# A gated DeltaNet and Conformer block on one core: the long convolution's accumulator moves into PSUM, the recurrence's products share a bank, and GpSimd's queue gets an order between heads

## The chip, the core and the metric

The kernel runs on one core of a Trainium2 chip. Five engines of that core matter here: TensorE (PE, with PEld for its weight loads), VectorE (DVE), ScalarE (ACT), GpSimd (POOL) and SyncE (SP), whose queue issues most of the DMAs. Each engine works through its own instruction queue in order and waits where an instruction needs a result that isn't there yet. PE's products land in PSUM, which the kernel uses as 8 banks of 128 x 512 fp32. The metric is device microseconds (us) of one execution; the profile shows one execution, and its granted clock is the share of TensorE's full clock that the chip gave.

## What is computed

One residual block on x of 512 frames by 1024 channels, in float32: an RMSNorm, one wide input projection, two token mixers in parallel (a gated delta rule with 8 heads of 128, and a Conformer convolution), gates that merge them, an output projection, then a SwiGLU channel mixer and a last RMSNorm. Cut to the parts that the change touches:

```python
h = rmsnorm(x, norm1_w); proj = h @ w_in              # q, k, v, z, beta, decay, glu, gates
qkv = silu(causal_depthwise_conv(q|k|v, dn_conv_w))   # 4 taps
# gated delta rule, per head, in chunks: with T = I + strict lower part of beta*k k^T*decay
#   solve T [u | w] = [v*beta | k*beta*exp(gc)], then chunk by chunk
v_new = u_c - w_c @ S
o_c   = q_dec_c @ S + attn_c @ v_new
S     = S * exp(g_last) + k_dec_c^T @ v_new
out_a = (rmsnorm(o) * silu(z)) @ dn_w_o
c     = ga * sigmoid(gb)
c     = causal_depthwise_conv(c, cm_dw_w) + cm_dw_b   # 31 taps, per channel
c     = silu(layernorm(c))                            # over the 1024 channels
out_b = c @ cm_w_pw2 + cm_b_pw2
x     = x + (gate_a * out_a + gate_b * out_b) @ w_out
x     = x + (silu(h2 @ w_gate) * (h2 @ w_up)) @ w_down
```

## The kernel before

Channels lie on the 128 partitions and the 512 frames along the free axis, so one column tile of a projection is a 128 x 512 result in one PSUM bank, summed over 8 blocks of 128 input channels (a k step). Every product of the big projections is split into a high and a low part of both factors and done as three matmuls (`split3`, line 113), so a column tile is 24 matmuls. `unit` (lines 92 to 105) loads the weights of a tile by an SP DMA, makes the high part on ACT (line 102) and the low part on DVE (line 104).

The first phase runs 60 column tiles of the input projection, as generators that yield after each k step: for each of the 8 heads k, q, v and z (`head`, lines 643 to 670), with 8 k steps of other tiles (`others`: GLU tiles, then gate tiles) after each head. The driver (lines 683 to 702) takes one k step at a time and counts them; between k steps it advances the running chains of small work. A framework then turns the program into one queue per engine by priority and by its own estimates of when things are ready; `behind` (lines 85 to 90) and `tc.issue_after` put instructions of a block behind a given earlier one on that one's engine. The queues are fixed before the kernel runs.

Each head's small work has three stages.

- `front` (lines 326 to 378), once k is there. On POOL: a power (line 339), the masked products `Un` (349) and `Ud` (366), and then a forward substitution in 16 x 16 blocks, 15 pairs of a multiply (`ytm`, line 375) and an add (`y`, line 377). Between them ACT copies blocks of `Un` out (354), DVE makes `cc` (357), and SP stores `cc` to DRAM and loads it back, spread over the partitions, as `U`, in 8 DMAs (359, 362); the substitution reads `U`. `decay` (315 to 324) has one POOL instruction more per head (320).
- `front2` (380 to 397), after v: `Vp`, the masked q k products `at` (DVE, line 390) and the norms of q (PE, line 395).
- `chain` (399 to 510), from k step 84 + 40 h on: the blocks' inverse is built up to 128 x 128 (lines 405 to 464; line 405 on ACT is the first reader of the substitution's `y`, line 407 on DVE reads that, line 414 on PE reads 407's result, line 426 on DVE makes `Xd` for line 438 on PE), then the recurrence over 4 chunks of 128 frames (470 to 504). A chunk has five products: k S (476), q S (480), the inverse times R (482), the state's update (487), and `at` times w (494). Products 476 and 487 go into tile `sp`, which has a bank of its own; the other three go into slices of tile `st`, another bank. DVE makes R (478) and the new state (492), ACT makes w (484) and the scaled q S, `Ae` (499), and DVE adds the output `o` (500). In chunk 0 the state and o are ACT copies (490, 496). Both tiles have a single buffer.

The long convolution, `conv31` (lines 539 to 548), runs 8 times, once per 128 channels: ACT writes the first tap into an SBUF tile `cv[i]` (541), and 30 DVE instructions (543) each add one tap to it; each reads `c` and the accumulator and writes the accumulator, all in SBUF. `background` (615 to 621) hands them to the framework at the lowest priority, every 40 k steps, so that they fill DVE's gaps; several convolutions can be under way at once, each in its own `cv` tile. Their sum over the channels is `sacc` (545 to 548).

`ln_mean` (559 to 573) takes that sum with a matmul (561), subtracts the mean from all 8 tiles and sums the squares; it is called at the end of the first phase (708). `ln_norm` (575 to 583) needs one more matmul (577), scales, and applies SiLU on ACT (583); it is called before tile 3 of the 8 column tiles of the attention output projection (732). After those the tiles are split (725, 726) and go through the convolution branch's output projection.

Banks of PSUM in the first phase: 3 for projections (`mm`), 2 for `front` (`g`), 1 for `chain` (`b`), 1 each for `sp` and `st`.

Of the kernel before, what the change touches and what calls it, by code (L numbers as in the profile page):

```python
# [1 line left out]

# [28 lines left out]
def block_kernel(ctx, tc, a):  # L31
    nc = tc.nc
    V, S, G, PE = nc.vector, nc.scalar, nc.gpsimd, nc.tensor
# [91 lines left out]
    cv = [kp.tile([P, T], F32, name="cv", bufs=KD) for _ in range(KD)]  # L125
    tp = keep.enter_context(tc.tile_pool(name="tp", bufs=2))

    ph1 = ctx.enter_context(ExitStack())
    psg = ph1.enter_context(tc.tile_pool(name="psg", bufs=2, space=PSUM))
    psb = ph1.enter_context(tc.tile_pool(name="psb", bufs=1, space=PSUM))  # L130
    pst = ph1.enter_context(tc.tile_pool(name="pst", bufs=2, space=PSUM))

    cs = []

# [191 lines left out]
    def front(h, kT, DT):  # L326
        sq = junk[:, 0:P]

        ss = gp.tile([P, 8, NT], F32, name="ss", bufs=5)
        ps = tok(kT, psg, "g")  # L330
        for n in range(NT):
            S.activation(sq, ps[:, n, :], AF.Square, accum_out=ss[:, 0, n:n + 1])
        kd = gp.tile([P, 3, P], F32, name="kd", bufs=3)
        for n in range(3):
            S.activation(kd[:, n, :], ps[:, n, :], AF.Copy, scale=kdf[:, n, h:h + 1])
        kk, rk, nk, nb2, b2 = ss[:, 3], ss[:, 4], ss[:, 5], ss[:, 6], ss[:, 7]
        V.tensor_scalar(out=kk, in0=ss[:, 0], scalar1=EPS, scalar2=None, op0=ALU.add)
        V.reciprocal(out=rk, in_=kk)
        G.tensor_tensor(out=nk, in0=kk, in1=root4, op=ALU.pow)
        V.tensor_tensor(out=nb2, in0=rk, in1=nbeta[:, :, h], op=ALU.mult)  # L340
        V.tensor_tensor(out=b2, in0=rk, in1=beta[:, :, h], op=ALU.mult)

        ps = psg.tile([P, 4, P], F32, name="g")
        for n in range(NT):
            PE.matmul(ps[:, n, :], kT[:, n, :], kT[:, n, :], start=True, stop=True)  # L345
        Un = gp.tile([P, NT, P], F32, name="Un", bufs=3)
        for n in range(NT):
            S.activation(Un[:, n, :], ps[:, n, :], AF.Copy, scale=nb2[:, n:n + 1])  # L348
        G.tensor_tensor(out=Un, in0=Un, in1=DT, op=ALU.mult)  # L349

        cp = gp.tile([P, NT, 32], F32, name="cp")
        for b in range(4):
            b32 = slice(32 * b, 32 * b + 32)
            S.copy(out=cp[b32], in_=Un[b32, :, b32])
        cc = gp.tile([P, NT, 16], F32, name="cc")
        S.activation(cc, cp[:, :, 0:16], AF.Copy, scale=mh1)
        V.scalar_tensor_tensor(out=cc, in0=cp[:, :, 16:32], scalar=mh2, in1=cc, op0=ALU.mult, op1=ALU.add)
        sc = dram.tile([8, 16, NT, 16], F32, name="sc")
        nc.sync.dma_start(sc.rearrange("b k n c -> (b k) n c"), cc)
        U = gp.tile([P, 16, NT, 16], F32, name="U", bufs=2)  # L360
        for b in range(8):
            nc.sync.dma_start(U[16 * b:16 * b + 16].rearrange("p k n c -> p (k n c)"),
                              sc[b].rearrange("k n c -> (k n c)").partition_broadcast(16))

        Ud = gp.tile([P, NT, P], F32, name="Ud", bufs=3)
        G.tensor_tensor(out=Ud, in0=Un, in1=mc.rearrange("p (a t) -> p a t", a=1).broadcast_to([P, NT, P]),
                        op=ALU.mult)


        y = gp.tile([P, NT, 16], F32, name="y", bufs=3)  # L370
        S.copy(out=y, in_=idc.rearrange("p (a c) -> p a c", a=1).broadcast_to([P, NT, 16]))
        for k in range(15):
            w = 15 - k
            tm = gp.tile([P, NT, 16], F32, name="ytm")
            G.tensor_tensor(out=tm[:, :, 0:w], in0=U[:, k, :, k + 1:],  # L375
                            in1=y[:, :, k:k + 1].broadcast_to([P, NT, w]), op=ALU.mult)
            G.tensor_tensor(out=y[:, :, k + 1:], in0=y[:, :, k + 1:], in1=tm[:, :, 0:w], op=ALU.add)  # L377
        return ss, kd, b2, Un, Ud, y

    def front2(kT, qT, vT, DT, ss):  # L380
# [18 lines left out]
    def chain(h, kT, qT, ss, kd, b2, Un, Ud, Vp, at, yq, zs):  # L399
# [68 lines left out]
        o = gp.tile([P, NT, P], F32, name="o", bufs=3)  # L468
        Sp = None
        for n in range(NT):  # L470
            pp = pst.tile([P, P], F32, name="sp", bufs=1)
            ps = pst.tile([P, 4, P], F32, name="st", bufs=1)
            if n == 0:
                R = Vp[:, 0, :]
            else:
                PE.matmul(pp, kT[:, n, :], Sp, start=True, stop=True)
                R = gp.tile([P, P], F32, name="R", bufs=3)
                V.scalar_tensor_tensor(out=R, in0=pp, scalar=negc[:, n, h:h + 1], in1=Vp[:, n, :],
                                       op0=ALU.mult, op1=ALU.add)
                PE.matmul(ps[:, 2, :], qT[:, n, :], Sp, start=True, stop=True)  # L480
                yield 3
            PE.matmul(ps[:, 1, :], Y[:, n, :], R, start=True, stop=True)  # L482
            w = gp.tile([P, P], F32, name="w", bufs=2)
            S.activation(w, ps[:, 1, :], AF.Copy, scale=b2[:, n:n + 1])
            yield 3
            if n < NT - 1:
                PE.matmul(pp, kd[:, n, :], w, start=True, stop=True)  # L487
                Sn = gp.tile([P, P], F32, name="S", bufs=2)
                if n == 0:
                    S.activation(Sn, pp, AF.Copy)  # L490
                else:
                    V.scalar_tensor_tensor(out=Sn, in0=Sp, scalar=egl[:, n, h:h + 1], in1=pp,
                                           op0=ALU.mult, op1=ALU.add)
            PE.matmul(ps[:, 3, :], at[:, n, :], w, start=True, stop=True)  # L494
            if n == 0:
                S.activation(o[:, 0, :], ps[:, 3, :], AF.Copy)
            else:
                Ae = gp.tile([P, P], F32, name="R", bufs=3)
                S.activation(Ae, ps[:, 2, :], AF.Copy, scale=egc[:, n, h:h + 1])
# [37 lines left out]
    sacc = tp.tile([P, T], F32, name="sacc", bufs=1)  # L537

    def conv31(i, c):
        acc = cv[i]  # L540
        S.activation(acc, c[:, 0:T], AF.Identity, scale=c31w[:, i, 0:1], bias=dw_b[:, i:i + 1])
        for k in range(1, 31):
            V.scalar_tensor_tensor(out=acc, in0=c[:, k:k + T], scalar=c31w[:, i, k:k + 1], in1=acc,  # L543
                                   op0=ALU.mult, op1=ALU.add)
        if i == 1:
            V.tensor_tensor(out=sacc, in0=cv[0], in1=cv[1], op=ALU.add)
        elif i > 1:
            V.tensor_tensor(out=sacc, in0=sacc, in1=cv[i], op=ALU.add)
# [94 lines left out]
    def head(h, done):  # L643

        k_ = yield from conv4(8 + h, "kT")
        close()
        q_ = yield from conv4(h, "qT")
        close()
        v = conv4(16 + h, "vT")
        for _ in range(2):  # L650
            next(v)
            yield
        DT = dts.pop(0)
        if h + 1 < H:
            dts.append(decay(h + 1))
        with behind():
            ss, kd, b2, Un, Ud, y = front(h, k_, DT)
        v_ = yield from v
        pz = yield from proj(24 + h)
        z_ = zall[:, h, :]  # L660
        S.activation(z_, pz, AF.Silu)


        def last():
# [4 lines left out]
        chains.append([count[0] + 5, last()])  # L669
        yield  # L670

    def others():
# [8 lines left out]
            yield  # L681


    done, ended, dts, convs, count, chains = [], [], [], [], [0], [[0, decays()]]
    rest = others()
    for h in range(H):
# [17 lines left out]
    for _, sc, e in ended:  # L704
        if not sc:
            scaled(*e)
        finish(*e)
    vacc = ln_mean()
    ph1.close()


# [17 lines left out]
    mas = []  # L729
    oh, ol = zip(*[split(zall[:, k, :]) for k in range(KD)])  # L730
    for j in range(KD):
        if j == 3:
            ln_norm(vacc)
        ps = psm.tile([P, T], F32, name="mm")
        col_tile(ps, a["wo"][j], oh, ol)
        ma = mp.tile([P, T], F32, name="ma", bufs=KD + 1)
        V.tensor_tensor(out=ma, in0=ps, in1=gate_of(j), op=ALU.mult)
        mas.append(ma)
# [331 lines left out]
```

## Time and profile before

| | |
|---|---|
| median of 3 runs | 1000.03 us (997.23 to 1003.04) |
| the profiled execution | 1000.16 us |
| its span, first to last instruction | 998.4 us |
| granted clock over the span | 0.987 |
| busy: PE, DVE, ACT, POOL | 963.2, 680.7, 508.4, 302.1 us |
| long convolution on DVE (line 543) | 240 instructions, 186.5 us, mean 803 ns |
| substitution on POOL (lines 375, 377) | 240 instructions, 57.3 + 53.1 us |
| DMA over the span | 138.49 MB, mean 139 GB/s |

Rows of a time line give start and duration in us, the engine, the line of the kernel, the operation, what it writes and reads (`out<-in`), the shape and, after x, how many of them are merged in the row; in square brackets stands the idle time of the engine before it and whom it waited for. A row of waits reads "who <- for whom: total us, times, longest". Busy times of PE overlap from one matmul to the next, so a matmul's duration is longer than the step from one to the next. PE counts an fp32 product as two matmuls, so the four products of a head's small step show as x8.

### The profile page before, as it was taken

What the parts mean: (1) busy time and instruction counts of PE and PEld (TensorE: products, weight loads), DVE (VectorE), ACT (ScalarE), POOL (GpSimd) and SP (SyncE); (2) the same over time, 40 slices, a digit from 0 to 9 for tenths busy, and PEclk for the clock granted to TensorE, in tenths of its full rate; (3) what the DMA queues carried; (4) which work ended last, traced back from release to release, by engine and by line L of the source; (5) the groups of instructions that cost most, each with busy time, mean ns of one, the idle gap of its engine ahead of it and who ended that gap; (6) DMA issues with size and microseconds to landing.
All of it is one profiled execution on the core that took longest, in us unless ns stands there. A gap on an engine that the chain in (4) does not pass through costs nothing.

```text
span 998.4 us, 13414 instructions
## 1 busy us (share of the span) xinstructions
PE 963.2 (96%) x4775; PEld 790.2 (79%) x4775; DVE 680.7 (68%) x1044; ACT 508.4 (51%) x1053; POOL 302.1 (30%) x410
## 2 busy tenths in 40 slices
PE   7999889999999999999999999999999999999995
PEld 5687778787887888888878888888888888888784
DVE  4879688899769769998487644643344546468963
ACT  6597366867777665533456322422222322356543
POOL 0423836273453633000040000143534332001412
PEclk9999989999999999999999999999999999999997
DMA  8233323223041222233644432356565664256562
GB/s 320 90 107 97 97 64 97 59 81 117 27 134 58 93 87 64 96 117 134 239 165 148 141 124 85 119 201 241 210 238 195 233 228 143 90 168 191 158 210 84
DMA packets 48290, 138.49 MB, mean 139 GB/s; under 512 B 7472, under 2 KB 9424, under 8 KB 45408
## 3 DMA queue, kind: packets, MB, share of 16 engines
q1 hardware_dynamic: 44016, 112.36, 34.4%
q0 software_dynamic: 3488, 24.17, 6.7%
q10 hardware_dynamic: 720, 1.11, 0.3%
q8 instruction: 37, 0.61, 0.3%
q14 instruction: 29, 0.24, 0.1%
HBM read 119.52 MB, written 18.10 MB: 138 GB/s over the span
## 4 chain that ended last, share of the span: by engine, by line
PE 80%; DVE 9%; POOL 4%; ACT 3%; issue 3%; DMA 1%; SPq 0%; POOLq 0%; ACTq 0%; DVEq 0%
PE mm L113 60%; PE w L113 11%; DVE cv L543 3%; DVE wlo L104 2%; DVE acc L299 1%; POOL Un L349 1%; POOL ytm L375 1%; PE g L345 1%; PE st L482 1%; PE st L494 1%; PE b L414 1%; PE b L420 1%; PE st L480 1%; PE sp L487 1%; ACT Un L348 1%
## 5 line engine op out<-in xcount | busy, mean ns | idle before, releaser
L102 ACT ACTIVATE whi<-raw 128x1024 fp32r<-128x1024 f32 x167 | 176.2, 1057 | 318.5 <-PE mm L113 185.9
L113 PE MATMUL mm<-hh,whi 128*128 128x512 f32 x816 | 328.6, 403 | 0.0
L113 PE MATMUL mm<-hl,whi 128*128 128x512 f32 x816 | 323.4, 396 | 2.3 <-POOL hl L228 1.6
L113 PE MATMUL mm<-hh,wlo 128*128 128x512 f32 x816 | 323.2, 396 | 0.7 <-DVE wlo L104 0.7
L104 DVE TENSOR_TENSOR wlo<-raw,whi 128x1024 fp32r<-128x1024 f32 x167 | 214.4, 1285 | 120.8 <-ACT whi L102 120.2
L543 DVE SCALAR_TENSOR_TENSOR cv<-c,c31w,cv 128x512 f32<-128x512 f32 x240 | 186.5, 803 | 2.1
L113 PEld LDWEIGHTS mm<-hl,whi 128*128 128x128 f32 x816 | 154.5, 189 | 33.0 <-POOL hl L228 2.9
L113 PEld LDWEIGHTS mm<-hh,wlo 128*128 128x128 f32 x816 | 154.2, 189 | 32.7 <-DVE wlo L104 1.1
L113 PEld LDWEIGHTS mm<-hh,whi 128*128 128x128 f32 x816 | 154.5, 189 | 28.7 <-ACT hh L227 0.2
L375 POOL TENSOR_TENSOR ytm<-U,y 128x60 f32<-128x60 f32 (+14 forms) x120 | 57.3, 477 | 44.9 <-DMA U<-sc 36.2
L883 DVE TENSOR_TENSOR fm<-mm,fsg 128x512 f32<-128x512 f32 x21 | 14.5, 692 | 64.9 <-PE mm L113 64.9
L377 POOL TENSOR_TENSOR y<-y,ytm 128x60 f32<-128x60 f32 (+14 forms) x120 | 53.1, 442 | 9.3
L299 DVE SCALAR_TENSOR_TENSOR acc<-mm,c4w,acc 128x511 f32<-128x511 f32 (+2 forms) x72 | 53.2, 739 | 1.3 <-ACT acc L296 0.8
L113 PE MATMUL mm<-yh,whi 128*128 128x512 f32 x128 | 50.6, 396 | 0.0
L113 PE MATMUL mm<-yh,wlo 128*128 128x512 f32 x128 | 49.8, 389 | 0.0
L113 PE MATMUL mm<-yl,whi 128*128 128x512 f32 x128 | 49.8, 389 | 0.0
L113 PE MATMUL w<-whi,fh 128*128 128x512 f32 (+1 forms) x115 | 45.3, 395 | 2.8 <-ACT whi L102 2.8
L113 PE MATMUL w<-wlo,fh 128*128 128x512 f32 (+1 forms) x115 | 45.5, 396 | 2.1 <-DVE wlo L104 2.1
L113 PE MATMUL w<-whi,fl 128*128 128x512 f32 (+1 forms) x115 | 45.0, 393 | 0.0
L791 POOL TENSOR_SCALAR ss<-ss 128x1 f32<-128x1 f32 x17 | 5.7, 336 | 128.6 <-ACT sg L789 116.2
L920 POOL TENSOR_TENSOR A<-A,u 128x512 f32<-128x512 f32 x4 | 6.2, 1578 | 101.9 <-ACT u L951 75.4
L509 POOL TENSOR_TENSOR ss<-ss,half 128x4 f32<-128x4 f32 x8 | 9.5, 1189 | 82.4 <-DVE ss L507 82.4
(288 smaller groups left out, 1506.7 us busy)
## 6 DMA issues: line engine op xcount, KB each, us to landing
raw<-in_win_dram SPq DMA_DIRECT2D x61, 512.0 KB, 3.3
raw<-in_wgu_dram SPq DMA_DIRECT2D x44, 512.0 KB, 3.4
wst<-in_wdn_dram POOLq DMA_DIRECT2D x11, 1024.0 KB, 5.6
wsum<-wst POOLq DMA_DIRECT2D x11, 1024.0 KB, 4.3
raw<-wsum SPq DMA_DIRECT2D x44, 256.0 KB, 3.3
raw<-in_wdn_dram SPq DMA_DIRECT2D x33, 256.0 KB, 3.0
A<-in_x_dram SPq DMA_DIRECT2D x8, 512.0 KB, 6.8
U<-sc SPq DMA_DIRECT2D x64, 64.0 KB, 2.4
```

Source lines behind the costliest of these rows:

```text
L102: marked(S.activation(hi[:, 0:n], raw[:, 0:n], AF.Copy), "unit")
L104: marked(V.tensor_tensor(out=lo[:, 0:n], in0=raw[:, 0:n], in1=hi[:, 0:n].bitcast(F32), op=ALU.subtract), "unit")
L113: marked(PE.matmul(ps, l, r, start=first and i == 0, stop=last and i == 2))
L299: marked(V.scalar_tensor_tensor(out=acc[:, s:], in0=ps[:, :T - s], scalar=c4w[:, j, k:k + 1], in1=acc[:, s:], op0=ALU.mult, op1=ALU.add))
L345: PE.matmul(ps[:, n, :], kT[:, n, :], kT[:, n, :], start=True, stop=True)
L348: S.activation(Un[:, n, :], ps[:, n, :], AF.Copy, scale=nb2[:, n:n + 1])
L349: G.tensor_tensor(out=Un, in0=Un, in1=DT, op=ALU.mult)
L375: G.tensor_tensor(out=tm[:, :, 0:w], in0=U[:, k, :, k + 1:], in1=y[:, :, k:k + 1].broadcast_to([P, NT, w]), op=ALU.mult)
L377: G.tensor_tensor(out=y[:, :, k + 1:], in0=y[:, :, k + 1:], in1=tm[:, :, 0:w], op=ALU.add)
L414: PE.matmul(ps[:, n, 0:16], Ud[:, n, :], xc[:, n, 0:16], start=True, stop=True)
L543: V.scalar_tensor_tensor(out=acc, in0=c[:, k:k + T], scalar=c31w[:, i, k:k + 1], in1=acc, op0=ALU.mult, op1=ALU.add)
L883: V.tensor_tensor(out=fm, in0=pu, in1=sg, op=ALU.mult)
```

## The change

1. The accumulator of `conv31` is a tile of a new PSUM pool `psc` with one buffer, in place of `cv[i]`. The first tap is written there by ACT, the 30 DVE instructions read and write it there, and one more ACT instruction copies the result to `cv[i]`.
2. The tile `sp` is gone; its two products go into slice 0 of `st`, so that all five products of a chunk share one bank. The order changes with it: q S comes right behind k S, ahead of R; `at` times w comes right behind the state's update, ahead of the new state. The bank that this frees is the accumulator's.
3. `front` of heads 1 to 7 is wrapped in `tc.issue_after` with the last add of the previous head's substitution: on POOL, all of the head's `front` comes after it. A local function `last` is renamed `second`, since `last` now names a list that holds that add.
4. `ln_mean` is called before tile 2 of the attention output projection, no longer ahead of it, and `ln_norm` before tile 5, no longer before tile 3.

```diff
-    pst = ph1.enter_context(tc.tile_pool(name="pst", bufs=2, space=PSUM))
+    pst = ph1.enter_context(tc.tile_pool(name="pst", bufs=1, space=PSUM))
+    psc = ph1.enter_context(tc.tile_pool(name="psc", bufs=1, space=PSUM))
...
-            G.tensor_tensor(out=y[:, :, k + 1:], in0=y[:, :, k + 1:], in1=tm[:, :, 0:w], op=ALU.add)
+            last[0] = G.tensor_tensor(out=y[:, :, k + 1:], in0=y[:, :, k + 1:], in1=tm[:, :, 0:w], op=ALU.add)
...
-            pp = pst.tile([P, P], F32, name="sp", bufs=1)
-            ps = pst.tile([P, 4, P], F32, name="st", bufs=1)
+
+            ps = pst.tile([P, 4, P], F32, name="st")
             if n == 0:
                 R = Vp[:, 0, :]
             else:
-                PE.matmul(pp, kT[:, n, :], Sp, start=True, stop=True)
+                PE.matmul(ps[:, 0, :], kT[:, n, :], Sp, start=True, stop=True)
+                PE.matmul(ps[:, 2, :], qT[:, n, :], Sp, start=True, stop=True)
                 R = gp.tile([P, P], F32, name="R", bufs=3)
-                V.scalar_tensor_tensor(out=R, in0=pp, scalar=negc[:, n, h:h + 1], in1=Vp[:, n, :],
+                V.scalar_tensor_tensor(out=R, in0=ps[:, 0, :], scalar=negc[:, n, h:h + 1], in1=Vp[:, n, :],
                                        op0=ALU.mult, op1=ALU.add)
-                PE.matmul(ps[:, 2, :], qT[:, n, :], Sp, start=True, stop=True)
                 yield 3
             PE.matmul(ps[:, 1, :], Y[:, n, :], R, start=True, stop=True)
...
             if n < NT - 1:
-                PE.matmul(pp, kd[:, n, :], w, start=True, stop=True)
+                PE.matmul(ps[:, 0, :], kd[:, n, :], w, start=True, stop=True)
+            PE.matmul(ps[:, 3, :], at[:, n, :], w, start=True, stop=True)
+            if n < NT - 1:
                 Sn = gp.tile([P, P], F32, name="S", bufs=2)
                 if n == 0:
-                    S.activation(Sn, pp, AF.Copy)
+                    S.activation(Sn, ps[:, 0, :], AF.Copy)
                 else:
-                    V.scalar_tensor_tensor(out=Sn, in0=Sp, scalar=egl[:, n, h:h + 1], in1=pp,
+                    V.scalar_tensor_tensor(out=Sn, in0=Sp, scalar=egl[:, n, h:h + 1], in1=ps[:, 0, :],
                                            op0=ALU.mult, op1=ALU.add)
-            PE.matmul(ps[:, 3, :], at[:, n, :], w, start=True, stop=True)
...
     def conv31(i, c):
-        acc = cv[i]
+        acc = psc.tile([P, T], F32, name="cps")
         S.activation(acc, c[:, 0:T], AF.Identity, scale=c31w[:, i, 0:1], bias=dw_b[:, i:i + 1])
         for k in range(1, 31):
             V.scalar_tensor_tensor(out=acc, in0=c[:, k:k + T], scalar=c31w[:, i, k:k + 1], in1=acc,
                                    op0=ALU.mult, op1=ALU.add)
+        S.activation(cv[i], acc, AF.Copy)
...
-        with behind():
+        with behind(), tc.issue_after(last[0].ins) if h else nullcontext():
             ss, kd, b2, Un, Ud, y = front(h, k_, DT)
...
-    vacc = ln_mean()
     ph1.close()
...
-        if j == 3:
+        if j == 2:
+            vacc = ln_mean()
+        if j == 5:
             ln_norm(vacc)
```

More of the change, by code (lines that the diff above doesn't have):

```diff
@@ L1 @@
-from contextlib import ExitStack, contextmanager
+from contextlib import ExitStack, contextmanager, nullcontext
 import concourse.bass as bass
@@ L661, in head, with second @@
         S.activation(z_, pz, AF.Silu)
-        def last():
+        def second():
             Vp, at = front2(k_, q_, v_, DT, ss)
@@ L667, in last @@
             yield 0
-        chains.append([count[0] + 5, last()])
+        chains.append([count[0] + 5, second()])
         yield
@@ L681, in take @@
             yield
+    last = [None]
     done, ended, dts, convs, count, chains = [], [], [], [], [0], [[0, decays()]]
```

## The prediction, before the result was known

> **What bounds the kernel now.** I read the busy table by 40 us first, then by 4 us where TensorE (PE) isn't full, then the waits there, then the time lines of GpSimd (POOL) and VectorE (DVE). On the page PE is busy for 96% of the span:
>
> ```profile
> PE 963.2 (96%) x4775; PEld 790.2 (79%) x4775; DVE 680.7 (68%) x1044; ACT 508.4 (51%) x1053; POOL 302.1 (30%) x410
> ```
>
> The 40 us table (columns: stretch, length, then busy time and count of PE, PEld, DVE, ACT, POOL; granted clock, DMA share, GB/s) says where the 4% are. In 520-560 PE does 178 products in 40 us, 0.225 us each, and that is full pace.
>
> ```profile
> 80.00:120.00 40.00, 36.12 (x167) 29.53 (x167) 31.63 (x47) 24.60 (x58) 24.08 (x45) 0.91 0.39 112
> 120.00:160.00 40.00, 36.61 (x199) 29.86 (x198) 32.94 (x63) 23.75 (x64) 14.98 (x26) 0.91 0.24 76
> 160.00:200.00 40.00, 38.83 (x235) 31.96 (x234) 36.90 (x70) 30.64 (x87) 20.12 (x34) 1.00 0.24 73
> 200.00:240.00 40.00, 39.06 (x232) 31.65 (x231) 37.50 (x69) 27.54 (x77) 22.40 (x35) 1.00 0.29 93
> 520.00:560.00 40.00, 40.00 (x178) 33.10 (x178) 27.82 (x35) 20.37 (x26) 0.00 (x0) 1.00 0.46 143
> ```
>
> So the change can win only in 76-160, where heads 0 and 1 start up: 7.3 us of idle PE in 80-160, and a clock of 0.91 over the same 80 us, another 7.2. At 4 us (same columns) four holes stand out, three of them with a slow clock behind:
>
> ```profile
> 76.00:80.00 4.00, 2.54 (x16) 1.96 (x14) 4.00 (x6) 3.94 (x9) 0.53 (x1) 1.00 0.00 0
> 80.00:84.00 4.00, 4.00 (x14) 3.21 (x14) 4.00 (x8) 3.00 (x5) 1.71 (x1) 0.69 0.33 96
> 112.00:116.00 4.00, 1.37 (x10) 1.32 (x10) 0.31 (x1) 2.31 (x8) 3.07 (x13) 0.96 0.02 4
> 116.00:120.00 4.00, 4.00 (x16) 3.34 (x16) 3.42 (x4) 2.99 (x5) 3.77 (x5) 0.61 0.17 45
> 124.00:128.00 4.00, 2.56 (x12) 1.79 (x11) 3.97 (x9) 1.11 (x3) 3.41 (x8) 1.00 0.41 133
> 128.00:132.00 4.00, 3.98 (x35) 3.50 (x35) 3.10 (x8) 3.89 (x9) 1.62 (x6) 0.67 0.00 0
> 132.00:136.00 4.00, 4.00 (x17) 2.94 (x17) 3.94 (x11) 3.84 (x8) 0.00 (x0) 0.50 0.00 0
> 148.00:152.00 4.00, 2.07 (x13) 1.38 (x11) 2.45 (x4) 2.92 (x11) 2.55 (x2) 1.00 0.00 0
> ```
>
> Who is waited for in them (waits of 40-165: total us, times, longest):
>
> ```profile
> ACT yb L405 <- POOL y L377: 9.2, 1, 9.2
> DVE xc L407 <- ACT yb L406: 5.5, 1, 5.5
> PE b L414 <- DVE xc L407: 2.6, 1, 2.6
> PE st L480 <- ACT o L496: 1.9, 1, 1.9
> PE b L438 <- DVE Xd L426: 1.5, 1, 1.5
> PE g L395 <- DVE at L390: 1.5, 1, 1.5
> ```
>
> **Part 1: GpSimd's order.** The DMA issues and POOL's time line (start, duration):
>
> ```profile
> 82.35 3.56 SPq L362 DMA_DIRECT2D U<-sc  x8
> U<-sc SPq DMA_DIRECT2D x64, 64.0 KB, 2.4
> 94.46 1.45 POOL L339 TENSOR_TENSOR ss<-ss,root 128x4 f32<-128x4 f32 x1 [9.48 <-DVE ss L337]
> 99.05 1.29 POOL L366 TENSOR_TENSOR Ud<-Un,cst 128x512 f32<-128x512 f32 x1
> 98.34 0.74 POOL L375 TENSOR_TENSOR ytm<-U,y 128x60 f32<-128x60 f32 x1
> 113.39 0.21 POOL L377 TENSOR_TENSOR y<-y,ytm 128x4 f32<-128x4 f32 x1
> 102.84 4.20 SPq L362 DMA_DIRECT2D U<-sc  x8
> 160.81 0.35 ACT L405 ACTIVATE yb<-y,cst 128x64 f32<-128x64 f32 x1
> ```
>
> Head 0's U is issued by 85.9 and lands 2.4 later, at 88.3, but POOL's next instruction is head 1's power (L339), which waits until 94.46; the substitution starts at 98.34 and ends at 113.6, 15.3 us, 1.3 of them Ud of head 1. With the change it starts at 88.3 and takes at most the same 14.0, so it ends by 102.3. ACT reached its wait for it at 113.6 - 9.2 = 104.4, so that wait goes, and with it DVE's 5.5 and PE's 2.63 (4 - 1.37). The slow clock behind (0.61 over 4 us: 1.56) goes too: -4.2. What is put behind: head 1's power, Un and Ud, up to 7.8 us later than now (102.3 against 94.5), and through Un its copies on ACT, its cc on DVE, and on SP the store and eight loads of U, with the weight loads queued after them. U of head 1 then lands by 117.2, not 109.4; its substitution, which had to wait for 113.6 anyway, starts up to 3.6 late and, at its 16 us or less, ends before 134, and ACT reads it only at 160.81 (the last row): that cover is wide. If a weight load is caught behind the store, the price is one such hole, 4 us; I put no price on it, since SP's queue is filled in the order in which things come ready. For heads 2 to 7 POOL is idle before their power, and nothing changes.
>
> The hole at 124-136 (1.44 idle; 0.67 and 0.50 of clock, 1.3 + 2.0) is PE behind DVE's queue, which starts late because of those 5.5 us. I credit half: -2.4.
>
> **Part 2: the convolution in PSUM.** One step of it, on DVE's time line, and the conv4 step, which reads PSUM (ns min/median/max):
>
> ```profile
> 67.56 10.85 DVE L543 SCALAR_TENSOR_TENSOR cv<-c,c31w,cv 128x512 f32<-128x512 f32 x10
> 447.26 2.07 DVE L543 SCALAR_TENSOR_TENSOR cv<-c,c31w,cv 128x512 f32<-128x512 f32 x3
> 456.92 4.68 DVE L543 SCALAR_TENSOR_TENSOR cv<-c,c31w,cv 128x512 f32<-128x512 f32 x6
> L299 DVE SCALAR_TENSOR_TENSOR acc<-mm,c4w,acc x72: 650/742/750, 46.9 to 354.9; 128x511 f32<-128x511 f32 x24, 128x510 f32<-128x510 f32 x24, 128x509 f32<-128x509 f32 x24
> L349 POOL TENSOR_TENSOR Un<-Un,DT x8: 1282/1299/2605, 73.0 to 356.1; 128x512 f32<-128x512 f32 x8
> ```
>
> Two convolutions taken in turn go at 0.665 us a step ((2.07 - 0.74)/2), one alone at 0.785 ((4.68 - 0.75)/5), ten beside POOL's work at 1.085. Steps that read PSUM never exceed 0.75, beside POOL or not. With one accumulator bank the convolutions can't alternate any more, so a step costs 0.785 everywhere, but none costs 1.7. No row has DVE writing to PSUM; between the rows 0.665 and 1.085 I take 0.79, the row of a lone chain. The ten steps ahead of L390 then take 7.9 in place of 10.85; the 1.46 of PE at 76-80 and its clock (1.24) go, up to 0.94 a step: -2.7. POOL no longer shares with these steps: Un of head 2, the 2.6 us one, takes 1.3, so ACT's copies and L496 behind them come 1.3 earlier, and of PE's 1.93 in 148-152 that goes: -1.3.
>
> By the Trainium skill (Perfetto Trace Analysis, Optimizing Scalar/DVE Operations) a DVE instruction has about 65 ns more of access overhead on PSUM than on SBUF, and a profiled latency shows about twice that. The 742 ns median of L299 shows none of it for reads; for writes no run here shows it. By that page I estimate 0.85 to 0.92 a step, and -2.7 would stand.
>
> Added: eight copies out of the bank by ACT, each like one of these (L725, seven in 4.71 us):
>
> ```profile
> 524.90 5.76 ACT L583 ACTIVATE cv<-cv,vec 128x512 f32<-128x512 f32 x8
> 539.81 4.71 ACT L725 ACTIVATE yh<-cv 128x512 fp32r<-128x512 f32 x7
> ```
>
> 5.4 us, on an engine busy for half the span; but each waits for the last DVE step, and the next first tap for the copy, with weight copies and evacuations queued behind on ACT. Free at best; at worst one wait like the 9.2 above, 4.2 of PE. I take +1.0.
>
> **Part 3: the mean and norm, two column tiles later.** That is 2 x 24 products x 0.225 = 10.8 us. SiLU ended at 530.7; now 541.5, and the splits that PE needs started at 539.8: 1.7 us late at worst plus a clock drop like those above (1.6), nothing at best. PE takes a k step in 0.675, ACT splits one in 0.67. I take +0.8. The mean itself hid behind full PE and saves nothing.
>
> **Part 4: the recurrence in one bank.** In
>
> ```profile
> L499 ACT ACTIVATE R<-st,sm 128x128 f32<-128x128 f32 x24 | 8.8, 367 | 4.2 <-PE st L494 3.9
> PE sp L487 <- ACT w L484: 1.6, 2, 1.2
> PE sp L476 <- ACT S L490: 1.3, 3, 0.9
> ```
>
> L499 reads slice 2 yet waits for the product into slice 3: users of one tile wait for each other. So R now waits for the qT product too, the new state for the at product (0.2 us a pair), and Ae for the state (0.37): 0.55 at 24 hand-overs, 13.2 at most. The next kT product waits for o, as qT beside it did already. In all 24 PE waits 1.9 + 1.6 + 1.3 = 4.8 now, so projection work covers most; from 0 to 13.2 I take +2.0, near the measured row.
>
> **The sum.** -4.2 - 2.4 - 2.7 - 1.3 + 1.0 + 0.8 + 2.0 = -6.8. The profiled execution took 1000.16 (span 998.4 and 1.8 around it), the median of three runs is 1000.03: 993.4 us.
>
> **The rivals.** *The clock isn't the holes' doing* (0.20): the drops stay, 1.56 + 1.65 + 1.24 = 4.45 of the gain; 997.8. For it: no drop follows the 1.93 at 148-152. The Trainium skill (TensorE: Matmul & The Clock Gate, Part 1) has the clock fall only after about 3.4 us idle; by it no hole here explains a drop. The trace disagrees so far: three of four holes, the longest 2.63, have one behind. *The holes move* (0.16): queue orders are written ahead, PE runs into the next late result and half of the 10.6 comes back; 998.7. *The bank is slow to write* (0.08): at 1.0 us a step the 45 convolution steps of 160-240 add 9.5 to DVE's 74.4 of 80 us: 3.9 over, and 2.7 and 2.4 are lost; 1002.4. It decides from 0.94. The 45:
>
> ```profile
> 160.00:200.00 40.00, 19.99 (x24) 1.00 0.24 73
> 200.00:240.00 40.00, 18.18 (x21) 1.00 0.29 93
> ```
>
> *The recurrence is bare* (0.10), the slower side: all 13.2 on PE in place of 2.0, and three clock drops of 1.6; 1009.4. It decides from 0.4 us a hand-over. For it: DVE at 93% in 160-240, each slot late; against: 4.8 us in 24 today.
>
> **How the numbers follow.** Forecast 0.46. A measurement of this kernel tells about 0.5%, 5 us, from no change: below 995.0, 995.0 to 1005.0, above. With all of the idle time and slow clock of 76-160 gone (7.3 + 7.2 + 1.5 at 76-80 = 16.0) and no cost the forecast would reach 984, which needs everything at once; with 1.7 us more cost than I put it leaves the faster side, so 0.04 of it is "same". Rivals one and two would be 994.0 and 994.9 if the three costs (3.8) were nothing: 0.08 of them is "faster". Faster 0.42 + 0.08 = 0.50; slower 0.10 and, with a step above 1.0 us, 0.02 of the slow bank, 0.12; same 0.38. The range of 985 to 1004 takes in the first three rivals and leaves out the bare recurrence.
>
> **What would show it.** Right: POOL's first substitution starts near 88 and ends by 102; ACT's 9.2 is gone; no convolution step above 0.95 us; PE idle in 76-160 under 4 us and the clock at 1.00 there; waits of L476 to L494 in sum under 8. Wrong: steps of 1 us, waits of L476 above 8, or the same clock rows with the holes gone.

## The result and the profile after

The kernel after took 987.52 us (median of four runs, 987.41 to 988.73); the kernel before, beside it, 999.25 us (997.23 to 1003.04). The ratio is 0.9881 (0.985 to 0.9912): 0.9% to 1.5% faster, 11.7 us where 6.8 were forecast. The sign and the range of 985 to 1004 held; the size was too small.

The two tables by stage, first before, then after (columns: stretch, length, busy time and count of PE, PEld, DVE, ACT, POOL; granted clock, DMA share, GB/s):

```profile
76.00:160.00 84.00, 75.27 (x379) 61.35 (x378) 68.57 (x114) 52.30 (x130) 39.59 (x71) 0.92 0.30 90
160.00:360.00 200.00, 196.87 (x1170) 160.63 (x1169) 168.02 (x318) 144.63 (x402) 102.76 (x173) 1.00 0.26 80
```

```profile
76.00:160.00 84.00, 82.67 (x471) 68.64 (x470) 72.09 (x126) 66.33 (x157) 42.48 (x101) 1.00 0.35 105
160.00:360.00 200.00, 194.08 (x1157) 159.20 (x1156) 158.26 (x312) 144.38 (x404) 64.13 (x150) 1.00 0.25 81
```

These two stages hold nearly all of it. In 76-160 PE's idle time fell from 8.73 to 1.33 us (7.4), and the clock rose from 0.92 to 1.00, 6.7 us over 84: 14.1 us. In 160-360 the idle time rose from 3.1 to 5.9: 2.8 us were given back. The net, 11.3, is most of the 12.6 by which the span of the profiled executions fell (998.4 to 985.8).

At 4 us (same columns), the stretches that the prediction named:

```profile
76.00:80.00 4.00, 4.00 (x26) 3.53 (x26) 2.48 (x4) 3.90 (x9) 2.15 (x2) 1.00 0.17 60
80.00:84.00 4.00, 4.00 (x19) 3.31 (x18) 3.99 (x6) 3.87 (x6) 1.38 (x1) 1.00 0.05 13
112.00:116.00 4.00, 4.00 (x20) 3.30 (x19) 4.00 (x7) 1.82 (x4) 0.00 (x0) 1.00 0.45 124
116.00:120.00 4.00, 4.00 (x20) 3.06 (x19) 2.21 (x7) 3.34 (x4) 3.17 (x8) 1.00 0.40 133
124.00:128.00 4.00, 4.00 (x28) 2.88 (x27) 2.65 (x7) 3.17 (x12) 2.31 (x11) 1.00 0.00 0
128.00:132.00 4.00, 4.00 (x22) 3.37 (x21) 4.00 (x10) 1.57 (x7) 1.01 (x1) 1.00 0.01 4
132.00:136.00 4.00, 3.58 (x16) 2.63 (x14) 2.95 (x6) 3.15 (x11) 2.58 (x2) 1.00 0.38 131
148.00:152.00 4.00, 4.00 (x30) 3.66 (x29) 3.01 (x6) 1.90 (x6) 3.21 (x12) 1.00 0.08 31
```

All four holes are gone but for 0.42 us at 132-136, and the slow clock with them. The longest of what PE still waits for in the small work between 40 and 380 us, in the view of waits:

```profile
PE st L477 <- ACT o L498: 5.3, 5, 1.2
...
PE g L396 <- ACT Vp L386: 1.0, 1, 1.0
...
PE b L415 <- DVE xc L408: 0.5, 1, 0.5
```

The first row is new, and it is the shared bank: at the hand-over from chunk 0 to chunk 1 of five heads, the next k S product cannot enter the bank until ACT has copied o out of it. Four of the five, 4.7 us, lie in 160-360. There all waits of the recurrence were 3.1 us before and are 4.9 now; the other 1.0 of the 2.8 is the second row, a product for the norms of q that waits for Vp. (Lines of the kernel after lie 1 to 5 below those of before: 415 is 414, 477 is 476.) The third row shows how narrow the first head's cover now is: the product that waited 2.6 us before is late by 0.5.

GpSimd's time line and the issue of U on SP (start, duration):

```profile
90.55 1.25 POOL L376 TENSOR_TENSOR ytm<-U,y 128x60 f32<-128x60 f32 x1 [8.43 <-DMA U<-sc]
...
102.19 0.21 POOL L378 TENSOR_TENSOR y<-y,ytm 128x4 f32<-128x4 f32 x1
102.35 1.02 POOL L340 TENSOR_TENSOR ss<-ss,root 128x4 f32<-128x4 f32 x1
103.34 1.71 POOL L350 TENSOR_TENSOR Un<-Un,DT 128x512 f32<-128x512 f32 x1
```

```profile
83.22 0.33 SPq L100 DMA_DIRECT2D raw<-in_win_dram  x1
83.60 5.13 SPq L363 DMA_DIRECT2D U<-sc  x8
```

The substitution ends at 102.4, as forecast, but by another way: it starts at 90.55 rather than 88.3, because SP begins the eight loads 1.25 us later, behind a weight load, and takes 5.13 us to issue them (3.56 before), and it lasts 11.9 us rather than 14.0, because its own instructions became quicker. The groups of before and then of after (busy us and mean ns of one stand behind the bar):

```profile
L543 DVE SCALAR_TENSOR_TENSOR cv<-c,c31w,cv 128x512 f32<-128x512 f32 x240 | 186.5, 803 | 2.1
L375 POOL TENSOR_TENSOR ytm<-U,y 128x60 f32<-128x60 f32 (+14 forms) x120 | 57.3, 477 | 44.9 <-DMA U<-sc 36.2
```

```profile
L545 DVE SCALAR_TENSOR_TENSOR cps<-c,c31w,cps 128x512 f32<-128x512 f32 x240 | 180.0, 750 | 4.9 <-ACT cps L543 1.0
L376 POOL TENSOR_TENSOR ytm<-U,y 128x60 f32<-128x60 f32 (+14 forms) x120 | 36.9, 307 | 60.6 <-DMA U<-sc 51.9
```

The convolution steps, the same but for the accumulator's place, no longer get in GpSimd's way: 477 ns became 307. (More than the place differs between these two kernels; conv_sbuf below, with the accumulator back in SBUF, has 447.) The Trainium skill (SBUF — State Buffer, Who interferes with whom) says that a DVE instruction with two inputs in SBUF contends with a GpSimd instruction that reads SBUF, as its second input comes by an interface that both share. The two rows agree with that; no run here looks at the interface itself.

### The profile page after: what moved, and what is told of

The parts are those of the page before. It is cut to its first block, busy times and chain, and to the rows that moved or that the text cites. A ratio compares the mean times of both kernels' runs of the same rounds, so it can differ in the third digit from the quotient of the medians.

```text
span 985.8 us, 13439 instructions
## 1 busy us (share of the span) xinstructions
PE 955.7 (97%) x4775; PEld 785.7 (80%) x4775; DVE 669.8 (68%) x1044; ACT 513.6 (52%) x1062; POOL 255.1 (26%) x410
## 4 chain that ended last, share of the span: by engine, by line
PE 84%; ACT 5%; DVE 4%; POOL 4%; issue 2%; DMA 1%; SPq 0%; POOLq 0%; ACTq 0%; DVEq 0%
PE mm L113 64%; PE w L113 11%; DVE wlo L104 1%; POOL Un L350 1%; ACT cp L355 1%; ACT Un L349 1%; PE st L477 1%; PE b L415 1%; PE b L421 1%; PE st L483 1%; POOL ytm L376 1%; PE st L489 1%; PE g L346 1%; DMA raw<-in_win_dram 1%; PE st L478 1%
## 5 line engine op out<-in xcount | busy, mean ns | idle before, releaser
L545 DVE SCALAR_TENSOR_TENSOR cps<-c,c31w,cps 128x512 f32<-128x512 f32 x240 | 180.0, 750 | 4.9 <-ACT cps L543 1.0
L300 DVE SCALAR_TENSOR_TENSOR acc<-mm,c4w,acc 128x509 f32<-128x509 f32 (+2 forms) x72 | 52.6, 738 | 1.5 <-ACT acc L297 1.2
L376 POOL TENSOR_TENSOR ytm<-U,y 128x60 f32<-128x60 f32 (+14 forms) x120 | 36.9, 307 | 60.6 <-DMA U<-sc 51.9
L378 POOL TENSOR_TENSOR y<-y,ytm 128x60 f32<-128x60 f32 (+14 forms) x120 | 34.9, 291 | 9.4
L864 POOL TENSOR_TENSOR wst<-wst 128x512 f32<-128x512 f32 x11 | 15.2, 1386 | 62.7 <-DMA wst<-in_wdn_dram 62.7
```

The lines of the kernel that those rows point to most:

```text
L300: marked(V.scalar_tensor_tensor(out=acc[:, s:], in0=ps[:, :T - s], scalar=c4w[:, j, k:k + 1], in1=acc[:, s:], op0=ALU.mult, op1=ALU.add))
L376: G.tensor_tensor(out=tm[:, :, 0:w], in0=U[:, k, :, k + 1:], in1=y[:, :, k:k + 1].broadcast_to([P, NT, w]), op=ALU.mult)
L378: last[0] = G.tensor_tensor(out=y[:, :, k + 1:], in0=y[:, :, k + 1:], in1=tm[:, :, 0:w], op=ALU.add)
L864: G.tensor_tensor(out=b11, in0=b12, in1=b11, op=ALU.subtract)
```

## The experiments

Eleven more kernels and the kernel after once more were timed, each beside the kernel before on the same chip; of holes there is a single execution. A trace shows one execution: those of share_only (1004.00 us), order_short (998.03), order_bank (997.71) and wait5y (988.41) lie at or near the upper end of their ranges, so what the shorter executions waited for isn't seen there. The first question was which part had brought the 11.7 us. Four kernels, measured on one chip, bear on it; the kernel before took 1000.44 us beside them (median of 35 runs). Theory O has it in GpSimd's order, theory P in the accumulator's place.

**order_only**: the kernel before with the order alone.

```diff
-        with behind():
+        with behind(), tc.issue_after(last[0].ins) if h else nullcontext():
             ss, kd, b2, Un, Ud, y = front(h, k_, DT)
```

> The kernel before, with the order between the heads on GpSimd alone. If that order is the cause (theory O): head 0's substitution starts when its U has landed, near 88 us, ScalarE's wait of 9.2 us for it goes, and with it the hole at 112-116, that at 124-128 and the slow clock behind both (4.2 + 4.8 us): 990 to 992 us; the holes at 77 and 148 stay. If the freed SBUF port is the cause (theory P): the substitution still runs beside convolution steps that read two SBUF tensors, and the sum moves by under 4 us: 996 or more.

Measured: 998.74 us, ratio 0.998 (0.9968 to 0.9992). Its stage, its longest wait of PE and GpSimd's time line:

```profile
76.00:160.00 84.00, 74.55 (x388) 60.30 (x387) 70.88 (x117) 54.64 (x136) 42.16 (x72) 0.96 0.32 91
```

```profile
PE g L395 <- ACT Vp L385: 5.4, 1, 5.4
```

```profile
88.97 0.29 POOL L375 TENSOR_TENSOR ytm<-U,y 128x60 f32<-128x60 f32 x1 [3.04 <-DMA U<-sc]
...
105.67 0.21 POOL L377 TENSOR_TENSOR y<-y,ytm 128x4 f32<-128x4 f32 x1
...
106.82 1.26 POOL L349 TENSOR_TENSOR Un<-Un,DT 128x512 f32<-128x512 f32 x1
```

The substitution starts 9 us earlier than before and takes 16.9 us, not "at most the same 14.0". Head 1's power and Un, now behind it, come at 105.8 and 106.8, and head 1's Vp stands behind both on ACT. One hole was exchanged for another, 5.4 us long.

**no_order**: the kernel after without the order.

```diff
-        with behind(), tc.issue_after(last[0].ins) if h else nullcontext():
+        with behind():
```

> The changed kernel without the order between the heads. Theory O: the substitution waits for the next head's power again, the hole near 112 and its slow clock are back: 994 to 997 us. Theory P: the substitution now runs at its undisturbed 12 us and ends before ScalarE needs it, whatever the order: 987 to 990 us.

Measured: 997.57 us, ratio 0.9966 (0.9954 to 0.9979).

```profile
76.00:160.00 84.00, 77.20 (x401) 63.80 (x401) 60.28 (x102) 58.18 (x141) 33.35 (x77) 0.92 0.33 98
```

```profile
PE b L415 <- DVE xc L408: 6.4, 1, 6.4
```

```profile
112.94 0.21 POOL L378 TENSOR_TENSOR y<-y,ytm 128x4 f32<-128x4 f32 x1
```

The substitution is quick, 11.8 us, but it starts behind head 1's work, at 101.4, and ends at 113.2, where it ended before.

**conv_sbuf**: the kernel after with the one accumulator in SBUF.

```diff
-        acc = psc.tile([P, T], F32, name="cps")
+        acc = tp.tile([P, T], F32, name="cps", bufs=1)
```

> The changed kernel with the convolution's one accumulator in SBUF in place of PSUM (one buffer, copied out as well), so that only the memory differs. Theory P: convolution steps of 1.7 us beside GpSimd's work are back, the substitution takes 14 to 15 us in place of 12, and holes on TensorE with slow clock return: 993 or more. Theory O: the order keeps the big holes shut, only those at 77 and 148 return, 2.7 + 1.3: 990 to 992 us. If the written order of the queues is all that counts, since it hardly changes here: 987 to 988 us.

Measured: 999.14 us, ratio 0.9996 (0.9981 to 1.0011).

```profile
L376 POOL TENSOR_TENSOR ytm<-U,y 128x60 f32<-128x60 f32 (+14 forms) x120 | 53.7, 447 | 59.6 <-DMA U<-sc 51.0
```

```profile
PE b L415 <- DVE xc L408: 4.8, 1, 4.8
```

```profile
108.65 0.21 POOL L378 TENSOR_TENSOR y<-y,ytm 128x4 f32<-128x4 f32 x1
```

With everything but the place, the substitution takes 16.6 us and ends at 108.9. Behind it come the next head's power and Un, ACT's copies of Un (at 111.1) and the second half of `yb` (at 113.6), and PE gets on at 114.4. One edit is not one difference, though, since the framework writes all queues anew: GpSimd's has the order of the kernel after up to 227 us, but DVE's differs from 62 us on, ACT's from 91 and PE's from 98. So the longer substitution can be put down to the place, as GpSimd does the same in the same order; the hole behind it is not wholly separated from the new order of the others.

Neither O nor P stands alone: no_order lies above the ranges of both. By the medians the order alone is worth 1.7 us, everything but the order 2.9, everything but the accumulator's place 1.3 (its interval takes in no change), and all together 11.7. The terms do not add.

**share_only**: the kernel before with the recurrence in one bank (part 4).

```diff
-                PE.matmul(pp, kT[:, n, :], Sp, start=True, stop=True)
+                PE.matmul(ps[:, 0, :], kT[:, n, :], Sp, start=True, stop=True)
+                PE.matmul(ps[:, 2, :], qT[:, n, :], Sp, start=True, stop=True)
```

> The kernel before, with the recurrence's five products in one bank, the other bank idle, and nothing else. If sharing costs the waits of the changed trace in 160-360 (idle there 5.9 us in place of 3.1): 1001 to 1004 us. If the hand-over is bare: 1008 or more. If the waits only take the place of others: 998 to 1000 us.

Measured: 1001.32 us, ratio 1.001 (0.9994 to 1.0026); its one long wait of this kind is

```profile
PE st L476 <- ACT o L497: 2.6, 1, 2.6
```

Before, q S waited 1.9 for the same copy. The time lies at the lower edge of the first expected range; the price is some tenths of a percent at most, and alone it cannot be told from nothing. Nor does the shared bank alone bring the idle time of the kernel after: in 160-360 it is 3.5 us here, 3.1 before and 5.9 after. The wait of k S for o in that stretch is 0.9 us here, 1.3 in no_order, 1.8 in after_long (below) and 4.7 in the kernel after, so what the bank costs hangs on the order of the queues too; why it is most in the kernel after was not tested.

From this came **theory D**: a due time. At about 105 to 108 us PE comes to the first head's chain and the second head's `front2`. What they need passes through GpSimd (the substitution, then power and Un) and through ACT's queue behind it. The order starts that chain ten us earlier, the PSUM accumulator makes it five shorter; either alone is too late and costs one hole of about 5 to 6 us with a slow clock behind it. Theory C is that what counts is the convolution's own steps. Two kernels move GpSimd's end and leave the rest.

**order_short**: order_only with a shorter substitution.

```diff
-        for k in range(15):
+        for k in range(0 if h else 5, 15):
```

> The kernel before with the new order of GpSimd alone, and with the first 5 of the 15 steps of head 0's substitution left out (that part of the computation is not done; nothing else differs from order_only, which took 998.7 us). Theory D (a due time: head 0's substitution and, behind it, head 1's power must be through by about 105 us, whatever makes them so): the substitution starts near 89 as in order_only and ends near 99 instead of 105.9, TensorE's hole of 5.36 us at 105.4 and the half clock at 110.6 to 117.5 (3.5 us) go, though the convolution is still in SBUF: 989 to 992 us. Theory C (the convolution steps themselves must be quicker; GpSimd's time is only a sign of that): a hole of the same kind stays or opens some us later, 995 to 999 us.

Measured: 994.28 us (989.62 to 998.17), ratio 0.995 (0.9933 to 0.9967), below order_only by 4.5 by the medians on two chips and by 3.0 by the ratios, and between the two expectations. In the trace the hole shrank and did not go; the second fence is ACT's time line:

```profile
PE g L395 <- ACT Vp L385: 2.4, 1, 2.4
```

```profile
104.01 1.22 ACT L354 COPY cp<-Un 32x128 f32<-32x128 f32 x4 [2.91 <-POOL Un L349]
105.25 0.60 ACT L661 ACTIVATE A<-mm 128x512 f32<-128x512 f32 x1
...
106.65 1.12 ACT L385 ACTIVATE Vp<-g,ss 128x128 f32<-128x128 f32 x4
```

ACT stands 2.91 us behind GpSimd's Un, and Vp behind that; Vp must empty a bank before PE's product L395 may enter it. In the kernel after Un is no earlier (it ends at 105.05, here at 103.98), but there L396 ran at 100.4, right behind DVE's `at` and before Vp, so it took the bank that `at` had emptied. So a part of it is which bank the plan gives to one product: theory B, taken up below.

**after_long**: the kernel after with a longer substitution.

```diff
-            G.tensor_tensor(out=tm[:, :, 0:w], in0=U[:, k, :, k + 1:],
-                            in1=y[:, :, k:k + 1].broadcast_to([P, NT, w]), op=ALU.mult)
+            for _ in range(3 if h == 0 and k < 7 else 1):
+                G.tensor_tensor(out=tm[:, :, 0:w], in0=U[:, k, :, k + 1:],
+                                in1=y[:, :, k:k + 1].broadcast_to([P, NT, w]), op=ALU.mult)
```

> The kernel after with the multiply of the steps 0 to 6 of head 0's substitution issued three times in place of once (the same values are written again): 14 more instructions of GpSimd, about 0.37 us each, 5.2 us. Theory D: the substitution ends near 107.6 instead of 102.4, head 1's power with it, and though the convolution is in PSUM a hole of 4 to 6 us of TensorE at 103 to 112 comes back with a stretch of half clock behind it: 993 to 998 us. Theory C (what counts is the speed of the convolution's steps): they stay at 0.75 us, and the time stays at 987 to 989 us.

Measured: 993.74 us (993.33 to 995.59), ratio 0.9941 (0.9925 to 0.9957). Its two stages, the end of the substitution, PE's wait and the clock:

```profile
76.00:160.00 84.00, 77.48 (x406) 63.58 (x406) 63.11 (x107) 59.71 (x143) 41.17 (x100) 0.94 0.31 99
160.00:360.00 200.00, 197.13 (x1183) 162.09 (x1182) 158.87 (x315) 147.96 (x409) 71.04 (x159) 1.00 0.25 80
```

```profile
108.70 0.21 POOL L379 TENSOR_TENSOR y<-y,ytm 128x4 f32<-128x4 f32 x1
```

```profile
PE b L416 <- DVE xc L409: 5.0, 1, 5.0
```

```profile
116.00:120.00 4.00, 4.00 (x15) 3.52 (x15) 2.81 (x5) 3.47 (x7) 1.08 (x1) 0.50 0.31 86
```

This is D's plainest case. GpSimd ends 6.5 us later (108.9 for 102.4), the convolution is untouched in PSUM, and a hole of 5.0 us with half the clock behind it comes back. The time is 6.2 us above the kernel after, 5.7 above ln_back (below) on the same chip. In 76-160 the loss is greater, about 9.4 us: 5.2 more idle time and 5.0 by the clock of 0.94, 0.8 of which lie inside the hole. But 3.0 come back in 160-360, where the idle time is 2.9 with the same shared bank. C, which gave 987 to 989, falls.

**order_bank**: order_only, with that one product in another bank.

```diff
-        ps = psg.tile([P, 4, P], F32, name="g")
+        ps = psb.tile([P, 4, P], F32, name="b") if len(done) == 1 else psg.tile([P, 4, P], F32, name="g")
```

> The kernel before with the new order of GpSimd (order_only, 998.7 us), and for head 1's second front part the sums of q squared go to the bank of tag b instead of one of the two banks of tag g. In order_only this product (L395) sits 5.36 us until ScalarE's Vp has emptied its bank, and Vp stands behind head 1's power and Un; in the kernel after the same product took the bank that VectorE's at had emptied, and waited for nothing. Theory D (GpSimd's due time, whichever bank is given out): the chain of the first head is as late as before, TensorE waits for xc some us later, hole and half clock move, 996 to 999 us. Theory B (order_only failed by the bank that the planner gave to one product): the 5.36 us and the 3.5 us of half clock behind it go, nothing else is late in 100 to 120, 989 to 992 us.

Measured: 995.25 us (993.17 to 997.71), ratio 0.9955 (0.9939 to 0.9971).

```profile
PE b L414 <- DVE xc L407: 2.2, 1, 2.2
PE b L420 <- ACT Q L416: 1.8, 1, 1.8
```

Between the two theories. The 5.4 us at L395 are gone, and 4.0 of them come back 7 and 11 us later, at 112 and 117, at the first head's chain: the hole moved, as D says, and shrank a little, as B says. Little else differs from order_only: GpSimd's queue has the same order, DVE's too up to 140 us. The bank's share of order_only's time is 2.5 us by the two ratios and 3.5 by the medians on the two chips; the intervals overlap at their ends, so this size is not settled.

**ln_back**: the kernel after with `ln_mean` and `ln_norm` at their old places (part 3).

> The kernel after with the mean and the norm of the LayerNorm back at their places of the kernel before (ahead of the first and of the fourth column tile of the output projection). Theory 1, the move costs and brings nothing: 987 to 988 us, no wait at the norm in either. Theory 2, the move was needed, since the convolutions now end at 479 instead of 470: TensorE's product for the mean waits for the last sum, 989 to 992 us, with a hole near 480 to 500. Theory 3, the later place cost what I put on it: 986.5 us or less.

Measured: 988.08 us (986.99 to 993.61), ratio 0.9893 (0.9871 to 0.9915). Neither kernel has a wait of PE in 470-560, though the last convolution step starts at 478.2 (478.8 in ln_back), where it was 469.2 in the kernel before. Part 3 costs and brings nothing that can be told.

**wait5** and **wait5y**: the kernel after with a wider first hand-over, and the same with two copies of Y. In wait5 the longer chain reads Y for the last chunk when the next head has begun to write it, so that chunk is computed from a partly overwritten Y; the instructions are the same.

```diff
-                yield 3
+                yield 5 if n == 0 else 3
```

> The kernel after with one number changed: at the recurrence's first chunk the hand-over after the state is 5 slots of other products instead of 3, so that the next kT product is queued two column-tile steps later. The waits of TensorE for ScalarE's copy of o (5.3 us in 5 waits) are those of the shared bank. Theory 1, they are too short a distance: the waits go and nothing is late for it, 983 to 986 us. Theory 2, the bank's other users take the wait over (R, w, the next state), or the heads end later: 987 to 989 us. Slower than 990 if the later end of each head delays the next one's start.

> wait5 (5 slots instead of 3 behind the state of the recurrence's first chunk), with two copies of the matrix Y that the heads take in turn: with one copy the longer chain reads Y for a head's last chunk when the next head has begun to write it. Theory 1, the waits of the first hand-over (5.3 us in 5 waits of the kernel after) are what the shared bank costs and are only a matter of distance: they stay away as in wait5 (1.9 us in 2 waits there), 984 to 986 us, 2 to 3.5 us below the kernel after. Theory 2, wait5 was short because its last chunks did not wait for their own Y: 987 to 989 us.

> The kernel after once more, unchanged, to stand on the same chip beside wait5y: 987 to 989 us.

Measured: wait5 985.09 us (984.0 to 986.06), ratio 0.985 (0.9833 to 0.9868); wait5y 985.66 us (984.12 to 988.41), ratio 0.9864 (0.984 to 0.9889); the kernel after, on the same chip as wait5y (after_again), 988.78 us (987.11 to 989.52). In wait5y PE's wait at the hand-over is

```profile
PE st L477 <- ACT o L498: 4.3, 5, 1.3
```

The "1.9 us in 2 waits" of the expectation came from a view that ended at 200 us; over all five waits wait5 has 4.4 and wait5y 4.3, and they lost only 1 of 5.3. So distance is not the cure, and theory 1 falls in its mechanism, though both times lie in its ranges. The two medians lie 2 to 3 us under the kernel after, the best of all here. wait5's range lies wholly below that of the kernel after, but its last chunks are computed from another Y; wait5y's overlaps it. In 160-360 the idle time of both is 4.6 and 4.7 us where it was 5.9; where the rest comes from stays open.

**holes**: the kernel after with eight made holes.

```diff
+            if f in gaps:
+                V.tensor_copy(out=gd, in_=fms[-1][:, 0:TH])
+                for _ in range(gaps[f]):
+                    V.scalar_tensor_tensor(out=gd, in0=gd, scalar=one, in1=gd, op0=ALU.mult, op1=ALU.max)
+                hold = tc.issue_after(PE.matmul(psw.tile([P, T], F32, name="w")[:, 0:TH], ident, gd, start=True, stop=True).ins)
```

> The kernel after with eight made holes of TensorE between 520 and 900 us: before every second product group of the first feed-forward loop one extra product (its result isn't used) waits for a chain of VectorE steps, one step longer each time. Lengths of about 0.5 to 6 us. Theory L (the length of a hole decides): all holes above one length have a half clock behind them, none below it; by the runs so far that length lies between 1.3 and 4.8 us. Theory A (the clock's own grid decides): of the holes between 1.4 and 2.8 us some have it and some do not, whatever their length, and the half clock lasts a multiple of 3.4 us.

Measured: 1046.01 us in the one execution. A hole of 3.04 us with nothing behind it and one of 4.18 us with half the clock, in the time line of PE and the table by 4 us:

```profile
685.34 0.70 PE L883 MATMUL w<-gd,cst 128*128 128x256 f32 x2 [3.04 <-DVE gd L882]
```

```profile
688.00:692.00 4.00, 4.00 (x19) 3.33 (x18) 0.00 (x0) 0.61 (x1) 0.54 (x1) 1.00 0.77 274
...
740.00:744.00 4.00, 2.43 (x6) 1.98 (x7) 1.35 (x3) 0.00 (x0) 1.67 (x2) 0.72 0.68 283
```

The made holes came out at 1.6 and 3.0 us (no drop) and at six lengths from 4.2 to 8.4 (a drop each). The traces of after and of after_again, the same program, show what length does not decide. Each has a hole of 1.05 us of L396 behind Vp near 181; after first:

```profile
180.00:184.00 4.00, 2.96 (x22) 2.54 (x21) 1.97 (x5) 2.69 (x12) 2.13 (x2) 1.00 0.12 39
184.00:188.00 4.00, 4.00 (x24) 3.39 (x23) 3.33 (x5) 3.76 (x11) 1.28 (x1) 1.00 0.12 34
```

```profile
180.00:184.00 4.00, 2.95 (x20) 2.43 (x19) 1.75 (x5) 3.13 (x11) 1.27 (x1) 0.98 0.22 74
184.00:188.00 4.00, 4.00 (x16) 3.38 (x15) 3.13 (x5) 3.13 (x9) 1.29 (x1) 0.59 0.08 19
```

One hole can be followed through the kernels: the 1.46 us at 78 us of the kernel before. With the accumulator in PSUM it is gone; in the five kernels with the accumulators of before it is there, 1.44 to 1.46 us long, with a half clock behind it in before and share_only and none in order_only, order_short and order_bank. Over all fourteen traces, holes of PE between 76 and 945 us: of 57 from 0.7 to 1.5 us 7 have a half clock within 5 us behind them, of 15 from 1.5 to 3.1 us 4, and all of 10 above 4 us.

## Why the prediction was right in sign and short in size

- *"it starts at 88.3 and takes at most the same 14.0, so it ends by 102.3"*, and with it the wait goes (part 1, −4.2). The end was right by luck, since both of its terms were off and the errors cancelled: 90.55 and 11.9. The 14.0 were taken without any help of part 2, and order_only measured 16.9, with the hole moved to head 1's Vp. The step that failed is that parts 1 and 2 were priced as separate terms: in these runs the hole goes only when both act. The prediction asked what comes behind the substitution, followed Un to ACT's copies and through `cc` to U of head 1, read at 160.8, and called that cover wide; it did not follow the copies to Vp and `yb` behind them in ACT's queue.
- *"I credit half: −2.4"* for 124-136. All of it went: the idle time of 76-160 fell by 7.4 where the terms held 6.1, and the clock gave 6.7 where they held 4.45. That is 3.5 us more in all, 2.4 of them the half that was not credited: the largest mis-sized term.
- *Part 2, −2.7 and −1.3.* Right for the kernel after: 76-80, 80-84 and 148-152 are full. The 1.46 of idle time goes with the place (holes, above); the 1.24 of clock behind it was there in two of five kernels with that hole, so a good share of that term is chance. The step was taken as 0.79; the rows gave a mean of 0.750, none above 0.757, and the lone chain kept its pace (below). Rival three falls. Its 9.5 us counts 45 steps from 0.79, but the rows that it adds them to hold them at 0.85 (19.99 + 18.18 = 38.17 us); from the rows it is 6.8, and DVE 1.2 over. The Trainium skill's extra time on PSUM (Perfetto Trace Analysis), 0.85 to 0.92 a step, is not seen.
- *Copies on ACT, +1.0, and part 3, +0.8.* Both nothing: no wait of PE stands behind the copies, and ln_back and the kernel after are alike.
- *Part 4, +2.0.* The recurrence's waits in 160-360 rose by 1.8, from 3.1 to 4.9; the other 1.0 of the 2.8 there is the product behind Vp. But share_only and after_long have no such rise in idle time, so that the size came near is partly luck. The place, o on ACT at the first hand-over, was named only as "as qT beside it did already". The bare recurrence did not come; DVE, on which rival four leaned, was busy for 158 of those 200 us, where it was for 168.
- *Rival one, the clock has its own reasons.* It falls for this change: no half clock is left in 76-160. *Rival two, the holes move*, is what happened in order_only, in order_bank and in conv_sbuf.

With the measured terms the sum is −14.1 + 2.8 = −11.3. Of the signs named beforehand all came but one: ACT's wait of 9.2 is gone, no step is above 0.757, PE's idle time in 76-160 is 1.33 and the clock 1.00, and the recurrence's waits are 5.5 in sum; the substitution ended by 102.4, but started 2.3 us late.

## What to carry to other kernels

When two parts of a change serve one late result, don't add their prices: find the time at which the waiting engine arrives, and ask of each part alone whether it makes that time. An instruction that is moved behind another in a queue takes along its readers' places in their queues, so follow it until an engine reads it that has nothing else to do. In this kernel accumulating in PSUM paid twice, on DVE and on the GpSimd that works beside it.

## What the runs showed of the hardware

A DVE chain that accumulates in PSUM ran as fast as one in SBUF, on the time line and in the group (ns min/median/max):

```profile
70.88 5.49 DVE L545 SCALAR_TENSOR_TENSOR cps<-c,c31w,cps 128x512 f32<-128x512 f32 x7
```

```profile
L545 DVE SCALAR_TENSOR_TENSOR cps<-c,c31w,cps x240: 709/750/757, 54.0 to 478.2; 128x512 f32<-128x512 f32 x120
```

Each step came 0.79 us after the last ((5.49 − 0.75)/6), as in SBUF (0.785), and the maximum fell to 757 ns. In conv_sbuf, one accumulator as well but in SBUF, it was 1833.

The half clock that follows a hole lasts 3.4, 6.8, 10.2 or 13.7 us in the traces' record of the clock, multiples of 3.4, and short holes bring it in some executions only. The Trainium skill (TensorE: Matmul & The Clock Gate, Part 1) has a window of about 3.4 us that runs free, which agrees with both; that a whole idle window is needed does not agree with the 11 holes of 0.9 to 2.6 us that have a drop behind them. So a short hole costs more than its length only now and then, at least 1.7 us (half of 3.4) when it does, and a hole above 4 us did so in all ten cases. In nine of these ten the half clock begins before the hole ends (in after_long at 112.8, the hole ends at 114.3), and what falls into the hole costs nothing more.
